# Second attention, first softmax: the best-keys rounds and the low parts of the last two projections' weights moved behind its normalisation on VectorE

## The chip, the cores and the metric

The kernel runs on one core of one Trainium2 chip. The metric is device time in microseconds (us) of the whole launch; the figure for a kernel is the median of several executions. TensorE is called PE (its weight loads PEld), VectorE DVE, ScalarE ACT, GpSimd POOL and SyncE SP.

## The reference, cut to what matters

A block of 256 tokens by 1024 columns passes through a first hybrid layer and then twice (l = 0, 1) through a second layer: attention of two kinds, an output projection with a layer norm, and a routed mixture of 16 experts. The change touches only the attention of the second layer. What it computes, cut down:

```python
proj = h @ w_in                      # split into qa, kva, kr, dq, dk, dv, iq, ik, iw
out_a = mla_group(...)               # 8 heads: softmax(q k^T) v, causal
# dsa_group, 8 heads, per query:
score = sum_heads relu(iq . ik) * iw     # causal
_, sel = lax.top_k(score, 64)            # n_keep = T // 4: the best keys
s = dq . dk[sel] * scale - slopes * dist
out_b = softmax(s) @ dv[sel]
return concatenate([out_a, out_b]) @ w_o
```

## The kernel before, in words

The 256 tokens are two tiles of 128 rows. Every matrix product that must keep float32 accuracy is done in three matmuls, from a high and a low part of each operand: `split` writes the high part on ACT (a rounding copy) and the low part, source minus high, with `lo_of` on DVE or on POOL (line 86 of the profile). The weights' low parts are `hl` tiles in the profile.

In each pass of the second layer, `layer(l)` runs these steps. `proj(0..10)` makes the first eleven column tiles of the input projection, `prep(i)` being the split of tile i's weights. `latent_stats`, `keys`, `values_` and `queries(g)` prepare the four pairs of latent heads. `mla_pair(j)`, j = 0..3, is scores plus `softmax_heads`, called here the first to the fourth softmax. Then `proj(11)` and `proj(12)` make the last two query tiles `dq` for the sparse heads (weights `wb`), `best_keys` finds the 64 best keys of a query in 8 rounds (a maximum of eight and a match-and-replace for each token tile: lines 936 and 937) and turns them into the mask `selm`, and `dsa_pair(j)`, j = 0..3, is the softmax of the sparse heads, which adds `selm` to the scores on PE. The output projection `wo_mm(k)`, k = 0..7, needs the heads of pair k and the split of `wo`'s rows k. Its four accumulators also take the transposed residual (line 83).

`softmax_heads` sets this chain: DVE takes the row maxima from the score sums in PSUM (L390) and scales them (L394); ACT does the exponentials with their sums (L397); DVE takes the reciprocal (L400) and multiplies the probabilities `P` (L402, one half of 128 columns and one of 256 for each head); PE transposes `P` (L406, six matmuls); ACT and DVE copy the transposes to SBUF (L409, L411); PE multiplies with the values (`sc<-P`); ACT and DVE split the result into `oh` and `ol`.

Each engine runs its instructions in the order of its queue, and waits at the first one that isn't ready. The order of each queue is chosen when the program is built, by a list scheduler that interleaves the steps. `with tc.issue_after(ins)` puts the instructions traced in its block behind `ins` on the engine of `ins`; on the other engines it changes nothing directly. `softmax_heads` returns two such marks: `most`, its last maximum (L390), and `first` (returned as `done`), its last multiplication of `P` (L402), both on DVE. The splits of `wo` already stand behind `first` of the first softmax.

`ring` is a ring of SBUF for weights: the first expert's gate weights (line 733) are loaded into the place of `wb`, so their loads wait until `wb` has been read for the last time. All weight loads are issued by SP, in one queue.

A third copy of the layer in the program runs only when an expert has over 64 tokens; it doesn't run here.

Of the kernel before, what the change touches and what calls it, by code (L numbers as in the profile page):

```python
# [34 lines left out]
def body(tc, a, out, dbg=None, upto=None):  # L35
    nc = tc.nc
    te, ve, se, ge, sy = nc.tensor, nc.vector, nc.scalar, nc.gpsimd, nc.sync
# [50 lines left out]
    def split(raw, shape=(1024,), eng=None, tile_=hl8, scale=1.0):  # L88

        t = tile_("hl", F32R, (128, 2, 1024))  # L90
        n = int(np.prod(shape))
        hi, lo = (t[:, i, 0:n] for i in range(2))
        if len(shape) == 2:
            hi, lo = (v.rearrange("p (a b) -> p a b", b=shape[1]) for v in (hi, lo))
        if raw is not None:
            se.activation(hi, raw, AF.Copy, scale=scale)  # L96
            HI["lo"] = lo_of(lo, raw, hi, eng)
        return hi, lo
# [700 lines left out]
    def layer(l, xT, xh, xl, general=False):  # L799
        ex = Experts(l)  # L800

        def wcol(c, n):
            for g, c0, c1 in (("wa", 0, 672), ("wb", 672, 1184), ("wd", 1184, 1312), ("wi", 1312, 1608)):
                if c < c1:
                    return W[f"{g}{l}"][:, :, c - c0:c - c0 + n]
# [17 lines left out]
        def pieces(ps, eng, sc):  # L823
            hi, lo = split(None, (KD, 128))
            for o, n, c in ps:
                se.activation(hi[:, :, o:o + n], wcol(c, n), AF.Copy, scale=sc)
                lo_of(lo[:, :, o:o + n], wcol(c, n), hi[:, :, o:o + n], eng)
            return hi, lo
# [9 lines left out]
        def prep(i):  # L838
            if i < len(tiles) and i not in WS:
                n, j, ps = tiles[i]  # L840
                eng = ge if l and i < 5 or i == 12 else ve
                b = 2 if i < 2 else 1
                sc = behind[:, b:b + 1] if l and i < 5 and not general else 1.0
                WS[i] = pieces(ps, eng, sc) if ps else split(wcol(C0[n] + 128 * j, 128), (KD, 128), eng, scale=sc)

        def proj(i, ahead=1):
            for q in range(ahead + 1):
                prep(i + q)
            if i not in PS:

                both = (0, 1) if i == 0 else (i,)
                for q in both:
                    PS[q] = A("prj", (128, T))
                for k in range(KD):
                    for q in both:
                        wh, wl = WS[q]
                        PS["last"] = mm3(PS[q], wh[:, k], wl[:, k], xh[:, k], xl[:, k], k == 0, k == KD - 1)
            n, j, _ = tiles[i]
            ps = PS[i]
            if n == "iq":  # L860
                se.activation(iq2[:, j, 0], ps, AF.Copy)
                lo_of(iq2[:, j, 1], ps, iq2[:, j, 0])
            elif n == "ikdk":
                for k2, p in ((ik2, ps[0:64]), (dk2, ps[64:128])):
                    for r in (slice(0, 64), slice(64, 128)):
                        se.activation(k2[r, 0], p, AF.Copy)
                        lo_of(k2[r, 1], p, k2[r, 0])
            elif n == "dq":
                se.activation(dq2[:, j, 0], ps, AF.Copy)
                lo_of(dq2[:, j, 1], ps, dq2[:, j, 0])  # L870
            elif n in dest:
                se.activation(dest[n](j), ps, AF.Copy)
            else:
                o = j + (3 if n == "kva" else 0)
                g = V(f"qn{l}" if n == "qa" else f"kvn{l}", j)
                se.activation(nh[:, o], ps, AF.Copy, scale=g)
                ve.scalar_tensor_tensor(out=nl[:, o], in0=ps, scalar=g, in1=nh[:, o].bitcast(F32), op0=ALU.mult, op1=ALU.subtract)
                se.activation(SQ[:, o], ps, AF.Square)
                if j == 1:
                    ge.tensor_tensor(out=SQ[:, o], in0=SQ[:, o], in1=SQ[:, o - 1], op=ALU.add)  # L880
# [52 lines left out]
        def best_keys():  # L933
            for r in range(8):
                for tt, (c, n) in enumerate(SPAN):
                    ve.max(out=m8[:, tt], in_=score[:, c:c + n])
                    ve.match_replace(out=score[:, c:c + n], in_to_replace=m8[:, tt], in_values=score[:, c:c + n], imm_value=-3e38)
            ve.tensor_scalar(score, score, -2e38, NEG, op0=ALU.is_gt, op1=ALU.mult)
            ve.tensor_tensor(out=selm, in0=score, in1=at.maskb, op=ALU.add)
# [72 lines left out]
        def mla_pair(j, S):  # L1012
            return softmax_heads(S, j, rn[:, 2], rn[:, 3, 0:2], lambda s, i: vm[:, s, (2 * j + i) * 64:(2 * j + i) * 64 + 64],
                                 oh[:, j], ol[:, j])
# [32 lines left out]
        first, most = mla_pair(0, S)  # L1047
# [4 lines left out]
        for j in (2, 3):  # L1052
            mla_pair(j, mla_scores(j))

        with tc.issue_after(most.ins):
            best_keys()
        for i in range(11, 13):
            proj(i)
        if not general:
# [360 lines left out]
    for l in range(2):  # L1420
        layer_loads(l)
        state = layer(l, *state)
        if state is None:
            break
        if dbg is not None and upto == f"xo{l}":
            sy.dma_start(dbg, state[0])
            break
    if dbg is None:

        need = nc.values_load(flag[0:1, 0:1], min_val=0, max_val=T)  # L1430
        with tc.If(need > 64):
            xT_ = act("xTg")
            xh_, xl_ = act("xhg", F32R), act("xlg", F32R)
            sy.dma_start(xT_, keep)
            se.activation(xh_, xT_, AF.Copy)
            lo_of(xl_, xT_, xh_)
            state = (xT_, xh_, xl_)
            for l in range(2):
                layer_loads(l, True)
                state = layer(l, *state, general=True)  # L1440
# [76 lines left out]
```

## Time and profile before

| what | value |
|---|---|
| median of 3 executions | 1060.44 us (1060.15 to 1061.89) |
| profiled execution | 1059.44 us |
| its span on the core | 1057.3 us |
| PE busy | 1019.1 us, 96% of the span |
| DVE busy | 531.4 us, 50% |
| ACT busy | 425.6 us, 40% |
| POOL busy | 76.6 us, 7% |
| mean granted clock of PE | 0.996 of full speed |

The profiled execution has its span and 2.1 us around it. Busy time is a mean over stages: the second layer's attention stands at about 405 to 470 us (l = 0) and 752 to 817 us (l = 1) of the span, each followed by the experts.

### The profile page before, as it was taken

The numbers are of one execution on the slowest core, as the hardware profiler recorded it, in microseconds if no ns is written. First come the engines' busy times: TensorE is split into PE (matmuls) and PEld (weight loads), VectorE is DVE, ScalarE is ACT, GpSimd is POOL, SyncE is SP. The second block draws the span as 40 slices with busy tenths as digits, with TensorE's granted clock in tenths as the row PEclk, the third lists the DMA queues.
The fourth block names the chain that finished last, engine by engine and source line by source line (L and its number), as shares of the span: only waits on it lengthen the run. The fifth ranks groups of instructions, "written<-read, shape, count | busy, mean of one in ns | idle before, by whom it ended". The sixth has DMA issues, their size and how long they took to land.

```text
span 1057.3 us, 16626 instructions
## 1 busy us (share of the span) xinstructions
PE 1019.1 (96%) x6768; PEld 730.1 (69%) x6768; DVE 531.4 (50%) x1010; ACT 425.6 (40%) x781; POOL 76.6 (7%) x80
## 2 busy tenths in 40 slices
PE   9999999999999999999899999999999999999995
PEld 7889999999999998775343434379877534343433
DVE  6775578977776679853110111147985402021104
ACT  5675548655554475542110111156654302011111
POOL 3500021000000010001000000032200200000001
PEclk9999999999999999999999999999999999999998
DMA  9933554765444244897999999985469799999995
GB/s 334 349 144 118 200 187 166 249 205 191 160 143 148 95 160 160 296 345 275 389 391 397 399 400 395 391 293 214 160 250 347 280 380 394 400 400 400 394 390 187
DMA packets 131796, 295.41 MB, mean 279 GB/s; under 512 B 6054, under 2 KB 36976, under 8 KB 125440
## 3 DMA queue, kind: packets, MB, share of 16 engines
q1 hardware_dynamic: 129936, 290.35, 74.9%
q0 software_dynamic: 1472, 3.40, 1.1%
q8 instruction: 55, 0.90, 0.3%
q10 hardware_dynamic: 304, 0.53, 0.1%
q14 instruction: 29, 0.24, 0.1%
HBM read 292.15 MB, written 2.10 MB: 278 GB/s over the span
## 4 chain that ended last, share of the span: by engine, by line
PE 85%; DVE 8%; ACT 4%; DMA 1%; issue 1%; POOL 1%; ACTq 0%; DVEq 0%; POOLq 0%
PE gu L74 21%; PE up L74 12%; PE pd L74 11%; PE fm L74 7%; PE prj L74 6%; PE yT L74 6%; PE tm L74 4%; PE wo L74 3%; PE pg L74 3%; PE sum L74 3%; PE sc L74 2%; DVE hl L86 2%; PE sc L406 1%; DMA wa<-in_w_in_dram 1%; ACT P L397 1%
## 5 line engine op out<-in xcount | busy, mean ns | idle before, releaser
L74 PE MATMUL gu<-e,xg 128*64 128x512 f32 x1024 | 226.9, 595 | 1.3 <-ACT sg L1303 1.3
L74 PEld LDWEIGHTS gu<-e,xg 128*64 128x64 f32 x1024 | 71.1, 137 | 134.7 <-issue 128.2
L74 PE MATMUL up<-h2h,hl 128*128 128x256 f32 x704 | 130.5, 283 | 0.0
L74 PE MATMUL pd<-e,aT 128*64 128x512 f32 (+1 forms) x544 | 115.0, 571 | 2.4 <-ACT aT L1318 2.3
L74 PEld LDWEIGHTS up<-h2h,hl 128*128 128x128 f32 x704 | 111.4, 192 | 0.0
L74 PE MATMUL up<-h2l,hl 128*128 128x256 f32 x352 | 99.7, 283 | 0.1
L74 PEld LDWEIGHTS pd<-e,aT 128*64 128x64 f32 x544 | 38.7, 137 | 71.3 <-issue 59.1
L86 DVE TENSOR_TENSOR y<-pd,y 128x512 fp32r<-128x512 f32 (+1 forms) x34 | 21.8, 657 | 104.3 <-ACT y L1334 104.3
L74 PEld LDWEIGHTS up<-h2l,hl 128*128 128x128 f32 x352 | 67.6, 192 | 0.3 <-DVE h2l L522 0.3
L1309 DVE SCALAR_TENSOR_TENSOR sg<-gu,gcol,sg 128x512 f32<-128x512 f32 x16 | 12.0, 751 | 110.0 <-PE gu L74 110.0
L1234 DVE TENSOR_REDUCE gcol<-pgt 64x1 f32<-64x2 f32 x32 | 5.0, 158 | 123.6 <-PE pgt L74 123.4
L74 PE MATMUL yT<-ac,hl 128*128 128x256 f32 x528 | 67.0, 283 | 0.1
L74 PEld LDWEIGHTS yT<-ac,hl 128*128 128x128 f32 x528 | 64.9, 192 | 0.3 <-ACT ac L642 0.3
L86 DVE TENSOR_TENSOR hl<-up,hl 128x1024 fp32r<-128x1024 f32 x44 | 53.8, 1225 | 19.5 <-ACT hl L96 19.4
L96 ACT ACTIVATE hl<-up 128x1024 fp32r<-128x1024 f32 x44 | 46.1, 1052 | 33.8 <-PE up L74 28.4
L1303 ACT ACTIVATE sg<-gu 128x512 f32<-128x512 f32 x16 | 9.6, 598 | 124.0 <-PE gu L74 124.0
L1334 ACT ACTIVATE y<-pd 128x512 fp32r<-128x512 f32 (+1 forms) x34 | 18.8, 571 | 96.1 <-PE pd L74 82.8
L1318 ACT ACTIVATE aT<-pact 128x512 f32<-128x512 f32 x16 | 9.6, 598 | 110.4 <-PE pact L1316 110.4
L74 PE MATMUL fm<-hh,hl 128*128 128x256 f32 x256 | 49.1, 288 | 0.9 <-ACT vu L323 0.9
L86 DVE TENSOR_TENSOR hl<-in,hl 128x1024 fp32r<-128x1024 f32 x32 | 38.6, 1219 | 11.2 <-ACT hl L96 11.0
L74 PE MATMUL wo<-hl,oh 128*128 128x512 f32 x128 | 43.9, 409 | 0.0
L74 PE MATMUL sum<-y,GT 128*128 128x512 f32 (+1 forms) x136 | 38.8, 404 | 3.0 <-ACT y L1334 1.6
(356 smaller groups left out, 2003.3 us busy)
## 6 DMA issues: line engine op xcount, KB each, us to landing
e<-in_w_up_dram SPq DMA_DIRECT2D x48, 1024.0 KB, 13.0
e<-in_w_down_dram SPq DMA_DIRECT2D x48, 1024.0 KB, 13.5
e<-in_w_gate_dram SPq DMA_DIRECT2D x40, 1024.0 KB, 14.5
e<-in_w_gate_dram SPq DMA_DIRECT2D x48, 512.0 KB, 10.8
up<-in_w_up_dram SPq DMA_DIRECT2D x22, 1024.0 KB, 5.2
e<-in_w_up_dram SPq DMA_DIRECT2D x32, 512.0 KB, 10.8
in<-in_w_in_dram SPq DMA_DIRECT2D x15, 1024.0 KB, 17.4
down<-in_w_down_dram SPq DMA_DIRECT2D x11, 1024.0 KB, 5.0
```

The lines of the kernel that those rows point to most:

```text
L74: return te.matmul(o, lhsT=l, rhs=r, start=start, stop=stop, skip_group_check=True)
L86: return (eng or ve).tensor_tensor(out=dst, in0=src, in1=hi.bitcast(F32), op=ALU.subtract)
L96: se.activation(hi, raw, AF.Copy, scale=scale)
L397: se.activation(P[:, i, c:c + n], S[:, i, c:c + n], AF.Exp, scale=scale if isinstance(scale, float) else scale[:, tt:tt + 1], bias=m[:, 1, ...
L406: te.transpose(S[:, i, 128 * b:128 * b + 128], P[:, i, 128 * b:128 * b + 128], ident)
L1234: ve.tensor_reduce(out=gcol[r, p:p + 1], in_=pt[r, x:x + 17:16], axis=AX.X, op=ALU.add)
L1303: se.activation(sg, psg, AF.Silu)
L1309: ve.scalar_tensor_tensor(out=sg, in0=psu, scalar=gcol[:, p:p + 1], in1=sg, op0=ALU.mult, op1=ALU.mult)
L1318: se.activation(aT, pt, AF.Copy)
L1334: se.activation(h_, ps, AF.Copy)
```

## The change

Three edits, which act in both passes. The low part of the weights of `proj(12)` goes from POOL to DVE. The weights' splits of `proj(11)` and `proj(12)`, which were made wherever the scheduler found room before those projections, have their DVE part behind the last multiplication of the first softmax. And `best_keys` stands behind that multiplication, where it stood behind the last maximum of the same softmax.

```diff
@@ prep
-                eng = ge if l and i < 5 or i == 12 else ve
+                eng = ge if l and i < 5 else ve
@@ after the four mla_pair calls
-        with tc.issue_after(most.ins):
+        with tc.issue_after(first.ins):
+            prep(11)
             best_keys()
+            prep(12)
         for i in range(11, 13):
             proj(i)
```

The scheduler makes new queues from this. The rows below are of the first pass; those of the second read alike.

The first place is DVE's queue at the first softmax, behind the last low part of the queries' weights (`hl<-qu`). `sc` is a score tile, `sm` holds a softmax's maxima and sums, `m` the eight best values of a round, `qx` the rotated queries. Before:

```order
L86 TENSOR_TENSOR hl<-wb_3904,hl 128x1024
L390 TENSOR_REDUCE sm<-sc 128x2 x2
L936 MAX m_3882<-score 128x8
L394 TENSOR_TENSOR sm<-sm,rn 128x4
L936 MAX m_3882<-score 128x8
L937 MATCH_REPLACE score<-m_3882,score 128x128
L937 MATCH_REPLACE score<-m_3882,score 128x256
L936 MAX m_3882<-score 128x8 x2
```

The change:

```order
L390 TENSOR_REDUCE sm<-sc 128x2 x2
L394 TENSOR_TENSOR sm<-sm,rn 128x4
L400 RECIPROCAL sm<-sm 128x4
L402 TENSOR_TENSOR P<-P,sm 128x2x128
L402 TENSOR_TENSOR P<-P,sm 128x2x256
L1001 TENSOR_TENSOR qx<-qp,at 128x512
L86 TENSOR_TENSOR hl<-wb_3904,hl 128x1024
L411 COPY P<-sc 128x384
L390 TENSOR_REDUCE sm<-sc 128x2 x2
L936 MAX m_3882<-score 128x8
```

The low part of `proj(11)`'s weights has moved from ahead of the maxima to behind the multiplication, and between the scaled maxima (L394) and the reciprocal (L400), where three rounds of best keys stood, nothing is left. The eight rounds now run between the second softmax's maxima and the fourth softmax's multiplication, all but the last match-and-replace.

The second place is the fourth softmax. First PE's queue around the transposes of its `P` (L406); `sc<-dk,dq` are the scores of the first sparse pair, `prj` is the last projection. Before:

```order
L74 MATMUL wo_4812<-hl,oh 128x512 x2
L74 MATMUL wo_4812<-hl,ol 128x512
L74 MATMUL wo_4813<-hl,oh 128x512
L74 MATMUL sc<-dk_3918,dq_3917 128x2x128 x6
L74 MATMUL sc<-dk_3918,dq_3917 128x256 x6
L406 MATMUL sc<-ident,P 128x128
L74 LDWEIGHTS SQ
L74 MATMUL sc<-at,SQ 128x384
L74 LDWEIGHTS SQ
L74 MATMUL sc<-at,SQ 128x384
L74 LDWEIGHTS identb
L74 MATMUL sc<-selm,identb 128x384
```

The change:

```order
L74 MATMUL sc<-dk_3918,dq_3917 128x2x128 x6
L74 MATMUL sc<-dk_3918,dq_3917 128x256 x6
L74 LDWEIGHTS SQ
L74 MATMUL sc<-at,SQ 128x384
L74 LDWEIGHTS SQ
L74 MATMUL sc<-at,SQ 128x384
L406 MATMUL sc<-ident,P 128x128 x6
L74 MATMUL prj<-xh_3818,hl 128x256 x2
L74 MATMUL prj<-xl_3819,hl 128x256
L74 MATMUL prj<-xh_3818,hl 128x256 x2
L74 MATMUL sc<-P,SQ 64x128 x6
```

Of the last projection's 24 matmuls 22 have moved from ahead of the fourth transposes to behind them; two, which need the high part alone, are still ahead. Eight of the sixteen residual transposes and two matmuls of the output projection have moved behind them too, and the two matmuls `sc<-at,SQ` of the sparse scores have come ahead. And DVE's queue from the fourth softmax's multiplication, in the change:

```order
L402 TENSOR_TENSOR P<-P,sm 128x2x128
L402 TENSOR_TENSOR P<-P,sm 128x2x256
L937 MATCH_REPLACE score<-m_3882,score 128x256
L86 TENSOR_TENSOR hl<-wb_3904,hl 128x1024
L411 COPY P<-sc 128x384
L938 TENSOR_SCALAR score<-score 128x384
L86 TENSOR_TENSOR dq_3917<-prj,dq_3917 128x256
L939 TENSOR_TENSOR selm<-score,at 128x384
L86 TENSOR_TENSOR hl<-wo_3906,hl 128x1024
```

The low part of `proj(12)`'s weights (`hl<-wb`), which POOL made at the time of the first softmax, and the mask `selm` now stand behind the fourth multiplication; before, `selm` stood ahead of it, and so did three low parts of `wo`, which are all behind it now.

The third place is SP's queue, where the first expert loads stand:

```order
+L744 DMA e_4788<-in_w_up_dram 128x4x512
+L744 DMA e_4790<-in_w_up_dram 128x4x512
 L733 DMA e_4780<-in_w_gate_dram 128x2x512
 L733 DMA e_4782<-in_w_gate_dram 128x2x512
 L733 DMA e_4784<-in_w_gate_dram 128x2x512
 L733 DMA e_4786<-in_w_gate_dram 128x2x512
-L744 DMA e_4788<-in_w_up_dram 128x4x512
-L744 DMA e_4790<-in_w_up_dram 128x4x512
```

The four gate loads of half a megabyte, which take the place of `wb`, now stand behind two loads of up weights, and wait for the low part that is made behind the fourth softmax.

## Rows read from the trace of the kernel before

**Rows 1.** The page: the span, and each engine's busy us, share and instructions.

```profile
span 1057.3 us, 16626 instructions
...
PE 1019.1 (96%) x6768; PEld 730.1 (69%) x6768; DVE 531.4 (50%) x1010; ACT 425.6 (40%) x781; POOL 76.6 (7%) x80
```

**Rows 2.** PE's waits in 400:470, then in 745:830: total us, times, longest.

```profile
PE sc L406 <- DVE P L402: 3.2, 4, 2.2
...
PE sc L406 <- DVE P L402: 2.1, 4, 1.1
```

**Rows 3.** PE's timeline, first pass: start us, us, instruction [idle before <-releaser].

```profile
406.47 0.39 PE L74 MATMUL sc<-at,identb 128*128 128x128 bf16 x4
...
411.20 1.48 PE L74 MATMUL sc<-kx,qx 128*128 128x128 f32 x8
414.86 0.30 PE L406 MATMUL sc<-ident,P 128*128 128x128 f32 x1 [2.19 <-DVE P L402]
...
419.20 0.40 PE L74 MATMUL prj<-xh,hl 128*128 128x256 f32 x2
419.44 0.28 PE L74 MATMUL prj<-xl,hl 128*128 128x256 f32 x1
...
431.79 1.31 PE L83 MATMUL wo<-ident,xT 128*128 128x128 f32 x10
432.86 0.71 PE L74 MATMUL wo<-hl,oh 128*128 128x512 f32 x2
...
435.19 0.30 PE L406 MATMUL sc<-ident,P 128*128 128x128 f32 x1 [0.25 <-DVE P L402]
```

**Rows 4.** DVE's timeline, first pass.

```profile
405.79 3.41 DVE L86 TENSOR_TENSOR hl<-wb,hl 128x1024 fp32r<-128x1024 f32 x1
409.12 1.01 DVE L390 TENSOR_REDUCE sm<-sc 128x2 f32<-128x256 f32 x2
...
430.84 0.55 DVE L939 TENSOR_TENSOR selm<-score,at 128x384 bf16<-128x384 f32 x1
431.30 0.75 DVE L86 TENSOR_TENSOR dq<-prj,dq 128x256 fp32r<-128x256 f32 x2
...
433.52 1.20 DVE L86 TENSOR_TENSOR hl<-wo,hl 128x1024 fp32r<-128x1024 f32 x1
434.63 1.02 DVE L402 TENSOR_TENSOR P<-P,sm 128x256 f32<-128x256 f32 x2
435.57 1.22 DVE L86 TENSOR_TENSOR hl<-wo,hl 128x1024 fp32r<-128x1024 f32 x1
```

**Rows 5.** POOL's timeline, the low part of the last projection's weights in each pass.

```profile
405.74 2.37 POOL L86 TENSOR_TENSOR hl<-wb,hl 128x1024 fp32r<-128x1024 f32 x1 [10.93 <-ACT hl L96]
...
753.45 3.46 POOL L86 TENSOR_TENSOR hl<-wb,hl 128x1024 fp32r<-128x1024 f32 x1 [10.65 <-issue]
```

**Rows 6.** DVE's timeline, second pass, at the first softmax.

```profile
755.70 1.22 DVE L394 TENSOR_TENSOR sm<-sm,rn 128x4 f32<-128x4 f32 x1
```

**Rows 7.** Windows: length, busy us by engine, clock, DMA share, GB/s.

```profile
410.00:420.00 10.00, 7.81 (x69) 7.07 (x68) 9.82 (x41) 8.08 (x22) 0.00 (x0) 1.00 0.60 213
...
430.00:440.00 10.00, 9.75 (x81) 7.69 (x80) 9.65 (x19) 5.21 (x15) 0.00 (x0) 1.00 1.02 384
...
480.00:490.00 10.00, 8.71 (x63) 5.80 (x61) 5.27 (x23) 1.13 (x2) 0.00 (x0) 1.00 0.49 156
```

**Rows 8.** ACT's timeline, first pass, at the first softmax's exponentials.

```profile
407.93 0.69 ACT L988 ACTIVATE SQ<-vps,rn 128x512 f32<-128x512 f32 x1 [2.26 <-PE vps L74]
410.43 0.46 ACT L397 ACTIVATE P<-sc,sm,rn 128x128 f32<-128x128 f32 x1 [1.81 <-DVE sm L394]
...
412.88 0.21 ACT L397 ACTIVATION_READ_ACCUMULATOR P<-sc,sm,rn 128x1 f32 x1
```

**Rows 9.** SP's timeline, first pass: the first expert loads.

```profile
409.26 1.90 SPq L733 DMA_DIRECT2D e<-in_w_gate_dram  x4
427.59 3.64 SPq L744 DMA_DIRECT2D e<-in_w_up_dram  x4
```

## The prediction, made before the change was run

> **What bounds the kernel now.** The page comes first: PE is busy for 1019.1 of a span of 1057.3 us [rows 1], so the kernel is as long as PE's work and PE's waits together, and a change to other engines counts only through the waits. The second view is the list of PE's waits over the second layer's attention. In each pass PE waits for one thing alone, the multiplication of `P` on DVE that the transposes need: 3.2 us in four waits in the first pass, 2.1 us in the second [rows 2]. That is all that this change can win, 5.3 us or 0.5%; what it can lose has no such end. Third, the timelines. The largest wait, 2.19 us, is at the first softmax, and another of 0.25 us at the fourth [rows 3]; so 3.2 - 2.19 - 0.25, about 0.7 us, belongs to the sparse pairs. Last, the windows: from 410 to 440 us DVE is busy for 9.7 to 9.8 us of every 10 shown, and PE for nearly as much except at that one wait [rows 7]. Two engines are full here, and the reader should keep both queues in sight.
>
> **Why PE waits at the first softmax.** DVE is late there. It makes the low part of `proj(11)`'s weights just ahead of the maxima, and that instruction takes 3.41 us, where an equal one later takes 1.1 to 1.2 [rows 4]. POOL makes the low part for `proj(12)` at the same moment, 405.74 to 408.11 [rows 5]. In the second pass POOL runs from 753.45 to 756.91, and a DVE instruction on four columns inside that time takes 1.22 us [rows 6]. So POOL's instruction costs DVE some 2.2 us in the first pass and about 1.1 in the second, which is also the difference between the two passes' waits.
>
> **What the change removes.** POOL's instruction is gone, and the low part of 1.1 us no longer stands ahead of the first maxima. These can then start when PE has the scores, at 406.47 + 0.39 = 406.9 [rows 3], instead of 409.12 [rows 4]: 2.2 us earlier. ACT's first exponential still stands behind a copy that begins at 407.93 and takes 0.69 [rows 8], so it starts at 408.6. The four exponentials, with a second such copy among them as before, took from 410.43 to 412.88 + 0.21 = 413.09, 2.66 us [rows 8]; now they end at about 411.3. The first `P` reaches PE at about 412 instead of 414.86, when PE has just come to it, so nearly all of the 2.19 us goes, and of the second pass's wait all but some 0.3.
>
> **What it adds to DVE.** Between the scaled maxima (407.9) and the end of the exponentials (411.3) DVE has nothing to do: three rounds of best keys stood there, and now nothing does. That is 3.4 us of an engine that is full until 440, and the work comes back later. What follows is the fourth multiplication, the last that PE needs before the sparse pairs. Before, DVE worked without a pause from the first maxima at 409.12 to the fourth multiplication at 434.63: 25.5 us [rows 4]. In the new queue this stretch has lost three low parts of `wo` (1.11 each, from 433.52 to 434.63: 3.3), the pass that writes `selm` (430.84 to 431.30: 0.46), two low parts of `dq` (0.7), and the pass before `selm` with the last match-and-replace; these two I estimate at 0.6, since each covers no more columns than the `selm` pass. It has gained one low part of `wb`, 1.1. So 25.5 - 3.3 - 0.5 - 0.7 - 0.6 + 1.1 = 21.5 us of work. The fourth multiplication starts at 406.9 + 21.5 + 3.4 = 431.8, and PE can use it 0.56 us later, as before (434.63 to 435.19) [rows 3, 4]: 432.4.
>
> **What PE has to do until then.** It is earlier than before by 2.8 us at this point, but PE has less to fill the time with. From 411.20 to the wait's start at 434.94 PE did 23.74 - 2.19 = 21.55 us of work [rows 3]. Of this the new queue has moved behind the fourth transposes 22 matmuls of the last projection (0.12 each, from 419.20 to 419.44 for two: 2.6) and 8 residual transposes (0.107 each, ten from 431.79 to 432.86: 0.9) [rows 3]; two matmuls of the output projection and two of the sparse scores change sides and are taken to cancel. That leaves 18.05 us, and PE is through at 429.25. Whatever small waits it meets on the way, it stands at the fourth transposes until 432.4: 3.1 us idle in all.
>
> **The second new wait.** The last projection needs the low part of its weights, which comes behind the fourth multiplication: both halves of `P` take 0.94 (434.63 to 435.57), the last match-and-replace about 0.4 (estimated as above), the low part 1.1 [rows 4]. It is ready at 431.8 + 2.45 = 434.3. PE's six transposes end at about 433.3, held by the second half of `P`; it waits 1.0. Behind the waiting projection in PE's queue stand the values of the fourth softmax, the mask matmuls and all the rest.
>
> **Sum.** New waits 3.1 + 1.0, plus the sparse pairs' 0.7, which I leave as it was: 4.8 us a pass. Against 3.2 in the first pass that is +1.6, against 2.1 in the second +2.7: +4.3 us. The profiled execution has 1057.3 us of span and 2.1 around it, 1059.4; it would become 1063.7. It lies 1.0 below the median of 1060.44, so the median becomes 1064.7, 0.4% more. The hand-offs that the sum leaves out, a wait from one round's result to the next instruction, are between 0 and 1.0 us a pass (DVE showed none before, and dependent pieces now stand closer); I take 0. The sparse pairs' waits lie between 0 and 1.5. The likeliest case's own range is 1061.5 to 1067.5.
>
> A rule of the Trainium skill (Perfetto Trace Analysis, section "Optimizing Scalar/DVE Operations") speaks against this edit by its first half: where DVE is saturated, some of its work may be better on ScalarE or even GpSimd; its second half says that moving work between GpSimd and DVE might not help, as they share a read port. The trace has both sides: DVE full, and a part on POOL that cost DVE 2.2 and 1.1 us where doing it costs 1.1 [rows 4 to 6]. By the first half alone, with the low part on POOL at a harmless time, the second new wait would go and the sum be 1.0 us less a pass, +2.3; by the rows as they stand, the edit to POOL's part is worth 0 to +1.1 us of DVE's time a pass, and the loss comes from the order.
>
> **Loads.** The first gate loads, issued at 409.26 before, now wait for the low part at 434.3, behind two up loads that go at about 427.6 [rows 9]. Two megabytes, 5.5 us at 384 GB/s, move from an idle stretch into a full one (DMA share 1.02 from 430). From 480 to 490 the DMA engines were busy for 0.49 of the time [rows 7], about 5 us free, so the rest of the loads come in time; I price this at 0.
>
> **Rivals.** *Faster*: DVE delivers the fourth `P` before PE needs it, and only the gain at the first softmax is left: about -1.9 in the first pass and -0.8 in the second, 1057.7. It decides from a fourth multiplication at 428.7, 3.1 us earlier than in my sum. For it: every multiplication is earlier than before. Against it: PE arrives earlier still, for the 3.5 us of moved matmuls. *No change*: the delay is taken up behind the attention, since the experts' loads run without pause after 490 and could set the stage's end alone; 1060.4. Against it: those loads wait around 480 to 490 for places that the end of the attention frees, so a late attention makes them late too. It also covers a fourth multiplication half-way between. *Slower still*: the two megabytes can't use that gap, since the loads that stood there come late as well; up to 5.5 us more a pass, 1075.7.
>
> **Chances.** Mine 0.62 (0.55 of it slower by over 0.2%, about 2.1 us, which is what a measurement of this kernel can tell from no change; 0.07 within); faster 0.17 (0.02 of it within); no change 0.15; slower still 0.06. Slower 0.61, within 0.24, faster 0.15. The range goes from 1057.5, which takes in half of the faster case, to 1068.5.
>
> **What would show it.** Right: the first wait of 2.19 gone to under 0.5, DVE idle for some 3 us ahead of the first reciprocal, PE waits of 2 to 3.5 us in front of the third and fourth softmaxes' transposes together and of about 1 us at `prj` for DVE's low part, and 4 to 6 us of PE waits in each pass. Wrong: a fourth multiplication before 429 (then DVE was not the limit), no wait at `prj`, or PE waiting for loads in the experts, which would say that the loads' new place matters.

## The result, and the profile after

| | before | after |
|---|---|---|
| median | 1060.61 us of 6 executions (1059.53 to 1061.89) | 1069.49 us of 6 (1066.76 to 1070.53) |
| profiled execution, its span | 1059.44, 1057.3 us | 1069.24, 1067.4 us |
| mean granted clock of PE | 0.996 | 0.990 |
| the attention, first and second pass | 71.68 and 70.58 us | 76.12 and 76.39 us |

The change costs 8.9 us: the ratio of after to before is 1.0081, 95% interval 1.0069 to 1.0092. The prediction was 1064.7 us in a range of 1057.5 to 1068.5: the direction was right, the size was not. Here "the attention" is the time from the first transposes of `prk` to the first transposes of `z` behind the layer norm, for after 476.20 - 400.08 and 827.89 - 751.50. It has grown by 4.44 and 5.81 us, 10.25 together, where the spans of the two profiled executions differ by 10.1: all of the loss is there. The rest of the span is 0.15 us shorter, which says little, since it is 915.0 us in one execution of the kernel before and 916.7 in another that is shown below; the medians, 8.9 apart, agree with the 10.25 to within that. A ratio here and below is worked out from the executions themselves and is not the quotient of the two medians (1.0084 here).

```profile
400.08 0.38 PE L960 MATMUL prk<-ident,rn 128*128 128x128 f32 x2
...
476.20 1.03 PE L772 MATMUL pt<-ident,z 128*128 128x128 f32 x8
...
751.50 0.38 PE L960 MATMUL prk<-ident,rn 128*128 128x128 f32 x2
...
827.89 0.82 PE L772 MATMUL pt<-ident,z 128*128 128x128 f32 x6
```

The page of after, its rows of PE: the same number of instructions, but 1026.7 us of busy time instead of 1019.1 [rows 1]. PE didn't only wait longer, it worked longer, and the clock's row shows two dips that the page of before hasn't got.

```profile
span 1067.4 us, 16620 instructions
...
PE 1026.7 (96%) x6768; PEld 735.2 (69%) x6768; DVE 530.2 (50%) x1012; ACT 425.3 (40%) x781; POOL 70.7 (7%) x78
...
PEclk9999999999999999899999999999989999999998
```

PE's waits of after from 400 to 470 us (us in total, times, longest), which answer to [rows 2]:

```profile
PE sc L406 <- DVE P L402: 2.2, 4, 1.4
PE sc L74 <- DVE ol L86: 0.9, 1, 0.9
PE prj L74 <- DVE hl L86: 0.8, 1, 0.8
PE sc L74 <- DVE P L411: 0.6, 1, 0.6
```

Four kinds of wait where there was one, 4.5 us where there were 3.2; the second pass has the same four, 4.5 where there were 2.1. DVE's timeline of after shows why; it answers to [rows 4]:

```profile
407.09 1.02 DVE L390 TENSOR_REDUCE sm<-sc 128x2 f32<-128x256 f32 x2 [1.03 <-PE sc L74]
...
411.39 0.18 DVE L400 RECIPROCAL sm<-sm 128x4 f32<-128x4 f32 x1 [3.08 <-ACT P L397]
...
432.13 1.02 DVE L402 TENSOR_TENSOR P<-P,sm 128x256 f32<-128x256 f32 x2
...
433.46 1.22 DVE L86 TENSOR_TENSOR hl<-wb,hl 128x1024 fp32r<-128x1024 f32 x1
```

The maxima start 2 us earlier, DVE stands idle for 3.08 us where the rounds had been, the fourth softmax's multiplication comes at 432.13, and behind it the low part of the last projection's weights. PE's timeline of after, which answers to [rows 3]:

```profile
412.17 0.30 PE L406 MATMUL sc<-ident,P 128*128 128x128 f32 x1 [0.17 <-DVE P L402]
...
428.04 0.88 PE L74 MATMUL sc<-P,SQ 128*64 128x128 f32 x12 [0.64 <-DVE P L411]
429.86 0.98 PE L74 MATMUL sc<-dk,dq 64*128 64x256 f32 x12 [0.94 <-DVE ol L86]
...
432.69 0.30 PE L406 MATMUL sc<-ident,P 128*128 128x128 f32 x1 [1.43 <-DVE P L402]
433.20 0.77 PE L406 MATMUL sc<-ident,P 128*128 128x128 f32 x5 [0.21 <-DVE P L402]
434.73 0.80 PE L74 MATMUL prj<-xh,hl 128*128 128x256 f32 x2 [0.76 <-DVE hl L86]
...
436.09 1.55 PE L74 MATMUL sc<-P,SQ 128*64 128x128 f32 x12
```

The first wait of 2.19 is down to 0.17. From 427.4 on PE waits five times within 7.3 us. Then look at the durations: the twelve matmuls `sc<-P,SQ` take 0.88 us at 428.04 and 1.55 at 436.09. The windows of one us show the reason (after the two bounds: width, PE busy, PEld, DVE, ACT, POOL, granted clock, DMA share, GB/s):

```profile
431.00:432.00 1.00, 0.27 (x2) 0.00 (x0) 1.00 (x6) 0.42 (x2) 0.00 (x0) 1.00 0.89 313
...
433.00:434.00 1.00, 0.77 (x5) 0.53 (x5) 1.00 (x4) 0.00 (x0) 0.00 (x0) 1.00 1.05 410
434.00:435.00 1.00, 0.27 (x1) 0.27 (x2) 1.00 (x2) 0.49 (x1) 0.00 (x0) 0.56 0.54 207
435.00:436.00 1.00, 1.00 (x5) 0.87 (x5) 1.00 (x4) 0.00 (x0) 0.00 (x0) 0.50 0.33 33
...
439.00:440.00 1.00, 1.00 (x7) 1.00 (x6) 0.66 (x1) 0.00 (x0) 0.00 (x0) 0.50 0.97 358
440.00:441.00 1.00, 1.00 (x7) 1.00 (x6) 0.00 (x0) 0.00 (x0) 0.00 (x0) 0.53 0.96 356
441.00:442.00 1.00, 1.00 (x11) 0.64 (x12) 0.20 (x1) 0.62 (x2) 0.00 (x0) 1.00 0.80 299
```

From 434.1 to 440.9 the granted clock is 0.50, 1.2 instead of 2.4 GHz, and PE, busy all the time from 435, gets through seven matmuls in each of the last two us, and through eleven in the first us after the clock is back. In the second pass's windows the same stands from 785.7 to 792.5. Before, the clock was 1.00 here [rows 7]. These windows are of one execution, but the fall is not that execution's alone: the mean granted clock of the whole span is 0.988 to 0.992 in all six executions of after, and 0.992 to 0.996 in the executions of the kernel before that were run beside the kernels below.

### The profile page after: what moved, and what is told of

Its sections match the earlier page's. It is cut to its first block, busy times and chain, and to the rows that moved or that the text cites. A ratio compares the mean times of both kernels' runs of the same rounds, so it can differ in the third digit from the quotient of the medians.

```text
span 1067.4 us, 16620 instructions
## 1 busy us (share of the span) xinstructions
PE 1026.7 (96%) x6768; PEld 735.2 (69%) x6768; DVE 530.2 (50%) x1012; ACT 425.3 (40%) x781; POOL 70.7 (7%) x78
## 4 chain that ended last, share of the span: by engine, by line
PE 78%; DMA 9%; DVE 7%; ACT 3%; issue 1%; POOL 1%; SPq 0%; ACTq 0%; DVEq 0%; POOLq 0%
PE gu L74 16%; PE up L74 12%; PE pd L74 8%; PE fm L74 7%; PE prj L74 6%; PE yT L74 6%; PE tm L74 4%; PE wo L74 4%; DMA e<-in_w_up_dram 3%; PE sc L74 3%; PE pg L74 3%; DMA e<-in_w_gate_dram 2%; DMA e<-in_w_down_dram 2%; PE sum L74 2%; PE qp L74 1%; PE sc L406 1%
## 5 line engine op out<-in xcount | busy, mean ns | idle before, releaser
L74 PE MATMUL prj<-xhn,hl 128*128 128x256 f32 x208 | 41.4, 296 | 2.2 <-POOL hl L86 1.0
```

The lines of the kernel that those rows point to most:

```text
L74: return te.matmul(o, lhsT=l, rhs=r, start=start, stop=stop, skip_group_check=True)
```

## The experiments

Theory A: the change costs some 2 us a pass in waits, as predicted, and nearly 3 more by the clock that falls behind them. Rival B: the new place of the gate loads, or the attention's new order itself, costs the time. Question C: what does each part of the change do alone? Lengths of the attention are taken as above from each kernel's profiled execution, of which there is one for each kernel; a median stands beside its ratio to the kernel before, run on the same chip (before's median lay between 1060.52 and 1060.86 us).

| kernel | attention, us | median, us | ratio (95%) |
|---|---|---|---|
| before | 71.68, 70.58 | 1060.6 | |
| after | 76.12, 76.39 | 1069.49 | 1.0081 (1.0069 to 1.0092) |
| after, all waits filled, transposes | 73.43, 73.63 | 1065.34 | 1.0037 (1.0026 to 1.0047) |
| after, all waits filled, matmuls | 73.42, 73.59 | 1066.50 | 1.0049 (1.0032 to 1.0066) |
| after, the fourth softmax's wait filled | 73.43, 73.61 | 1065.54 | 1.0039 (1.0026 to 1.0053) |
| after, the other waits filled | 74.61, 74.86 | 1065.74 | 1.0050 (1.0036 to 1.0063) |
| before, gate loads late | 71.64, 70.57 | 1063.19 | 1.0021 (1.0010 to 1.0032) |
| engine's part alone | 69.53, 69.55 | 1057.11 | 0.9960 (0.9946 to 0.9973) |
| order's part alone | 71.75, 71.73 | 1062.70 | 1.0013 (1.0003 to 1.0023) |
| both low parts behind the first softmax, rounds not | 70.78, 70.78 | 1060.47 | 0.9994 (0.9984 to 1.0003) |
| low parts first, then the rounds | 71.46, 71.47 | 1061.52 | 1.0004 (0.9993 to 1.0016) |

**All waits filled.** The fillers are put into PE's finished queue, ahead of the instructions at which it waits, so that no other instruction changes its place (`u`: ahead of the third softmax's products with the values; `v`: behind them; `t`: ahead of the fourth softmax's transposes; `p`: ahead of the last projection's third matmul; `warm` is the instruction that is copied, here a transpose of the identity).

```diff
+            FILLS.append((MARK["p"], (u, 5, 0), (v, 8, 1), (t, 12, 0), (MARK["p"], 6, 0)))
...
+            for _ in range(count):
+                f = copy.replace(warm, name=nc.get_next_instruction_name(), outs=[copy.replace(o, offset=o.offset + 256, ap=warm.outs[0].ap)])
+                code.insert(at, f)
```

> The changed kernel with 31 transposes of the identity a pass put into PE's own waits (5, 8, 12 and 6 of them, into a free half of the last projection's bank): they compute nothing that is used, every other instruction keeps its place. Theory A (the waits cost 3.9 us and the fall of the granted clock to 0.50 behind them about 6): PE has no cluster of waits left, the granted clock stays at 1.00 from 430 to 445, the projection's matmuls go at 0.12 us again instead of 0.21, and the time is 1063 to 1064.5, 3 to 4 above the kernel before. Rival B (the loads' new place, or the attention's new order itself, costs the 9 us and the clock only marks where PE waits): 1069 to 1070, as the change. If the clock stays up and the time is still 1069, A falls.

Measured: 1065.34 us, 0.8 above the expected range, and the attention is 2.69 and 2.76 us shorter than after's, with the clock at 1.00 in it. The waits are no shorter, they are only full: the fourth softmax's multiplication starts 32.07 us behind the first transposes of `prk`, in after 32.05. (This kernel's sums are not those of after: its fillers probably spoil the first two products of the last projection, which no run tested by itself.) So I repeated it with other fillers, copies of the last projection's second matmul, `q`:

```diff
+            FILLS.append((MARK["q"], (u, 5, 0), (v, 7, 1), (t, 11, 0), (MARK["p"], 6, 0)))
```

> The changed kernel again with fillers in PE's waits, here 29 extra matmuls a pass (5, 7, 11 and 6, each a copy of the last projection's second matmul at 0.12 us) into the unused half of that projection's bank; nothing that is used changes, and every other instruction keeps its place. Theory A, with the size that the first filled kernel gave (waits +1.7 and +3.1 over the attention's two passes, the clock 2.7 us a pass): clock 1.00 from 430 to 445, attention 63.7 and 63.9 us long instead of 66.4 and 66.7, 1064 to 1066. If the first filled kernel gained because its transposes spoiled part of the projection, this one is back at 1069.

(The expectation counts the attention from a later mark; its 66.4 and 63.7 us stand for 76.1 and 73.4 here.) Measured: 73.42 and 73.59 us, the same within 0.04. The median is 0.5 above the expectation. More work on PE makes the changed kernel faster by 0.3 to 0.4%: that shows the clock's share, 2.7 to 2.8 us a pass, and it refutes B's second half: the order is that of after, and the time is not.

**One place filled, and its complement.** The two edits are against the kernel with all waits filled with matmuls.

```diff
-            FILLS.append((MARK["q"], (u, 5, 0), (v, 7, 1), (t, 11, 0), (MARK["p"], 6, 0)))
+            FILLS.append((MARK["q"], (u, 0, 0), (v, 0, 1), (t, 11, 0), (MARK["p"], 0, 0)))
```

> The same fillers in one place only: 11 matmuls ahead of the fourth softmax's transposes, where the longest wait (1.43 us) is; the waits of 0.64, 0.94 and 0.76 us stay open. Theory A1 (any long wait of the cluster lowers the clock): it stays at 1.00 once the longest is filled, 1064 to 1066. Theory A2 (the waits count together, however they are divided): 2.5 us of waits within 7 us are still left, the clock falls for part of the time or not at all, between 1065 and 1069. Rival B: 1069.

Measured: 73.43 and 73.61. Its windows, and below them its waits from 400 to 470 us, show a PE that still stands idle for 3 us, at full clock throughout:

```profile
433.00:434.00 1.00, 0.79 (x6) 0.53 (x5) 1.00 (x4) 0.00 (x0) 0.00 (x0) 1.00 1.01 393
434.00:435.00 1.00, 0.24 (x2) 0.18 (x2) 1.00 (x2) 0.49 (x1) 0.00 (x0) 1.00 0.61 234
435.00:436.00 1.00, 1.00 (x13) 0.87 (x15) 1.00 (x4) 0.00 (x0) 0.00 (x0) 1.00 0.28 31
```

```profile
PE sc L93 <- DVE ol L105: 0.9, 1, 0.9
PE sc L425 <- DVE P L421: 0.8, 3, 0.4
PE prj L93 <- DVE hl L105: 0.8, 1, 0.8
PE sc L93 <- DVE P L431: 0.6, 1, 0.6
```

This is the cleanest measure of the terms. It leaves 3 us of true waits open, the attention is 1.75 and 3.03 us longer than before, and after is 2.69 and 2.78 us longer still (the clock's price). The 1.75 and 3.03 are not all waits. The windows of the whole attention, first pass, of before, of after and of this kernel:

```profile
399.89:471.57 71.68, 68.43 (x504) 55.80 (x503) 57.85 (x144) 36.77 (x100) 2.37 (x1) 1.00 0.73 269
400.08:476.20 76.12, 71.54 (x504) 58.51 (x503) 56.78 (x145) 36.80 (x100) 0.00 (x0) 0.96 0.63 233
400.17:473.60 73.43, 70.15 (x515) 57.46 (x514) 56.72 (x145) 36.84 (x100) 0.00 (x0) 1.00 0.66 241
```

PE idles for 71.68 - 68.43 = 3.25 us before and for 76.12 - 71.54 = 4.58 in after, so the waits cost 1.3 us (2.4 in the second pass). Here it idles for 3.28, as the fillers work in the other 1.3; without them 68.85 us of work are left, 0.4 more than before at the same clock (0.55 in the second pass). That is PE's own work in its new order, and what makes it longer isn't settled. So the first pass's 4.44 us are 1.33 of waits, 0.40 of the order and 2.71 of the clock, and the second's 5.81 are 2.44, 0.55 and 2.82. The medians of after and of this kernel differ by 4.0 us, where the attentions differ by 5.5; that, too, is within what the rest of the span varies by.

```diff
+            FILLS.append((MARK["q"], (u, 5, 0), (v, 7, 1), (t, 0, 0), (MARK["p"], 6, 0)))
```

> The complement of the kernel with one filled place: fillers in the three shorter waits (5, 7 and 6 matmuls into 0.64, 0.94 and 0.76 us), none ahead of the fourth softmax's transposes, where 1.43 and 0.21 us stay open. Theory A1 (the long wait alone lowers the clock): it falls as in the change, attention 4.4 and 5.8 us longer than before, 1069. Theory A2 (only the waits together do it, as the kernel before, with one wait of 2.19 us, shows no fall): clock at 1.00, attention 1.7 and 3.0 us longer, 1064 to 1066.

Measured: neither. The attention is 2.93 and 4.28 us longer than before, and the clock falls for half as long, from 432.2 to 435.6:

```profile
431.00:432.00 1.00, 0.27 (x1) 0.14 (x1) 1.00 (x4) 0.00 (x0) 0.00 (x0) 1.00 0.87 322
432.00:433.00 1.00, 0.79 (x5) 0.76 (x5) 1.00 (x4) 0.00 (x0) 0.00 (x0) 0.59 1.05 410
433.00:434.00 1.00, 1.00 (x6) 1.00 (x5) 0.71 (x1) 0.40 (x1) 0.00 (x0) 0.50 0.53 205
434.00:435.00 1.00, 1.00 (x6) 1.00 (x6) 0.87 (x3) 0.10 (x1) 0.00 (x0) 0.50 0.12 27
435.00:436.00 1.00, 1.00 (x9) 0.86 (x9) 1.00 (x3) 0.00 (x0) 0.00 (x0) 0.70 0.92 276
```

In these profiled executions the wait of 1.42 us alone brings a short fall, all waits together a long one, the short ones alone none. But before has a wait of 2.19 us in this stage and no fall. So neither the longest wait nor their sum decides by itself; what does stays open. The median, from five executions, is no higher than that of the filled kernels; here only the profile tells them apart, and whether every execution has the short fall isn't shown: the mean granted clock of the span is 0.993 to 0.995 in the five, and 0.993 to 0.996 in those with the fourth softmax's wait filled.

**The loads' place, by itself.** In the kernel before, the first gate load of each pass waits for a later value of DVE's semaphore.

```diff
+        load = next(i for i in code if type(i).__name__ == "InstDMACopy" and str(i.outs[0].memref).startswith(tile_name))
+        code[code.index(load)] = copy.replace(load, sync_info=copy.replace(load.sync_info, on_wait=[
+            copy.replace(w, wait_value=count) if w.ant_name.startswith("DVE") else w for w in load.sync_info.on_wait]))
```

> The kernel before with one wait made longer: the first of the four gate loads of each pass waits on DVE for the fourth softmax's multiplication (434.6 instead of 409.3 us), so the four loads, and the up loads queued behind them, are issued where the change issues the gate loads or later. Nothing else moves. Theory A: within 1 us of 1060.6, since the stretch from 480 to 490 us has 5 us of idle DMA time. Rival B (the loads' place costs): 2.5 to 5.5 us a pass, 1066 to 1071.

Measured: 1063.19 us, more than A allows and less than B asks for. SP's timeline of this kernel shows that the loads are as late as meant, the up loads far later than in the change:

```profile
436.71 1.90 SPq L754 DMA_DIRECT2D e<-in_w_gate_dram  x4
438.72 6.19 SPq L765 DMA_DIRECT2D e<-in_w_up_dram  x4
```

The attention has its old length, and between 470 and 760 us PE's list of waits is that of before, with no load in it. From the first transposes of `z` to the second pass's transposes of `prk` it takes 749.43 - 472.54 = 276.89 us instead of 275.96, and behind the second pass's first transposes of `z` 1.5 us more; in both stretches the clock falls to 0.50, from 506.9 to 510.3 and from 855.1 to 858.5 us, where the profiled execution of before has 1.00.

> The kernel before once more, for the spread between executions of one program. The kernel with the late loads lost 0.9 and 1.5 us outside the attention, where its clock fell to 0.50 at 506 and near 850 us behind waits that the kernel before has too. If that belongs to executions and not to the loads, this execution may show such a fall as well, with a time of up to 1063; if it shows none, the cause stays open.

Measured: 1061.54 us, ratio 1.0007 (0.9996 to 1.0017), and this execution does show the fall at 506. First its windows of two us, then those of the kernel before:

```profile
504.00:506.00 2.00, 0.74 (x4) 0.56 (x4) 1.04 (x2) 0.29 (x1) 0.00 (x0) 1.00 1.02 378
506.00:508.00 2.00, 1.64 (x4) 0.49 (x6) 0.47 (x2) 0.31 (x1) 0.00 (x0) 0.61 1.02 377
508.00:510.00 2.00, 2.00 (x8) 0.68 (x6) 0.00 (x0) 0.00 (x0) 0.00 (x0) 0.53 1.04 400
510.00:512.00 2.00, 2.00 (x12) 0.60 (x10) 0.00 (x0) 0.00 (x0) 0.00 (x0) 1.00 1.05 379
```

```profile
502.00:504.00 2.00, 1.30 (x8) 0.14 (x2) 0.56 (x1) 0.00 (x0) 0.00 (x0) 1.00 1.02 325
504.00:506.00 2.00, 1.07 (x6) 0.76 (x8) 0.95 (x3) 0.60 (x1) 0.00 (x0) 1.00 0.96 322
506.00:508.00 2.00, 2.00 (x12) 0.70 (x10) 0.00 (x0) 0.00 (x0) 0.00 (x0) 1.00 1.01 367
```

PE is busy for 10.37 of the 12 us from 500 in both; in one execution the clock falls behind the gap, in the other not. So such a fall needs no late loads. That they make it more frequent (2.2 us on average, by the ratio) was not excluded. For the change itself B's first half is out as the price of the attention: the filled kernels have the late gate loads (434.83 us with the fourth wait filled, 434.74 in after), and their attention's loss is that of the waits and of PE's order. Behind the attention a cost of up to about 2 us is not excluded.

**The parts alone.**

```diff
-                eng = ge if l and i < 5 or i == 12 else ve
+                eng = ge if l and i < 5 else ve
```

> One part of the change alone: the low part of the last projection on DVE instead of GpSimd; the best keys' rounds stay behind the first maxima. Theory A: the low part of projection 11 takes 1.1 us instead of 3.4, the maxima start 2.2 us earlier, the first wait of 2.19 (1.09) us nearly goes, DVE stays full, no cluster of waits, granted clock 1.00: 1056 to 1058.5. Rival C (DVE is full, so another 1.1 us on it comes back as a wait at the fourth softmax or at the projection): 1059.5 to 1061.5.

Measured: 1057.11 us, faster than before by 0.40%. DVE's timeline, and then PE's only wait of the first pass:

```profile
406.35 1.22 DVE L86 TENSOR_TENSOR hl<-wb,hl 128x1024 fp32r<-128x1024 f32 x1
407.48 1.01 DVE L390 TENSOR_REDUCE sm<-sc 128x2 f32<-128x256 f32 x2
...
424.65 1.20 DVE L86 TENSOR_TENSOR hl<-wb,hl 128x1024 fp32r<-128x1024 f32 x1
```

```profile
PE sc L406 <- DVE P L402: 0.4, 1, 0.4
```

The low part of projection 11 takes 1.22 instead of 3.41 us [rows 4], the maxima follow at once, and the rounds fill the time in which ACT does the exponentials. The other low part, 1.2 us at 424.65, delays nobody. The attention is 2.15 and 1.03 us shorter; the waits were 3.2 and 2.1 [rows 2] and are 0.4 and 0.4. The gate loads are issued at 426.35 us here, 17 later than before, and the kernel is faster all the same.

The order's part alone is the change with the condition `or i == 12` put back:

> The other part alone: rounds and the low part of projection 11 behind the first normalisation, the low part of projection 12 left on GpSimd at its old time. The wait at the projection for DVE goes, and its 24 matmuls can stand ahead of the fourth transposes again; DVE still idles for some 3 us. Theory A: waits of 2 to 4 us a pass in all, fewer of them close together, so the clock stays at 1.00 or falls for less time: 1059 to 1064. If the waits are as after and the clock falls as after, 1067 to 1069. Rival B (loads): the gate loads go at 409 again, so the time is that of before, 1060, whatever the waits do.

Measured: 1062.70 us, attention +0.07 and +1.15, the clock at 1.00 in it. PE's waits are 1.8 us a pass, none over 0.8. The last projection's weights are ready early here, and its matmuls stand ahead of the fourth transposes, in the place of the largest wait. So the waits are shorter than before's 3.2 and 2.1, and yet nothing is won: by the windows of the attention PE is busy for 69.86 and 69.84 us with the same matmuls, where it was for 68.43 in each pass. The loss of this kernel is PE's own work in another order, 1.4 us a pass.

Two other orders, with both low parts on DVE:

```diff
         with tc.issue_after(first.ins):
             prep(11)
-            best_keys()
             prep(12)
+        with tc.issue_after(most.ins):
+            best_keys()
```

> Both low parts of the last projections behind the first normalisation on DVE, as in the change, but the best keys' rounds back behind the first maxima, so that they fill DVE's idle 3.2 us. Theory A: DVE is full, no cluster of waits, the clock at 1.00: 1055.5 to 1058.5, as the kernel with the engine's part alone (1057.1). Rival: the low parts come late for PE, which reaches the projections by 415 us, and PE waits there for 1 to 2 us a pass: 1059 to 1061.

Measured: 1060.47 us, a miss: no change. The rival's time came, but not its waits. Only 0.35 us of waits a pass are left, yet the attention gains 0.90 us in the first pass and loses 0.20 in the second. With no more wait than the kernel with the engine's part alone it takes 1.2 us longer a pass. The windows of the attention, first pass, here and with the engine's part alone, say where:

```profile
401.66:472.44 70.78, 70.27 (x504) 55.96 (x502) 56.29 (x145) 36.66 (x100) 0.00 (x0) 1.00 0.68 249
400.45:469.98 69.53, 69.09 (x504) 56.02 (x503) 56.62 (x145) 36.52 (x100) 0.00 (x0) 1.00 0.67 247
```

The same matmuls at the same clock keep PE busy for 1.2 us longer. Its queue is interleaved in another way, with the last softmax's values at 466.7 us instead of 461.1; why that costs PE time wasn't settled.

```diff
             prep(11)
-            best_keys()
             prep(12)
+            best_keys()
```

> The change with the second low part ahead of the rounds instead of behind them. DVE still idles for 3.2 us, but the last projection's matmuls can stand ahead of the fourth transposes and fill PE's time. Theory A: the wait at the projection goes, the fourth multiplication stays late by about 1 us, 1.5 to 3 us of waits a pass, not close together, clock at 1.00: 1060 to 1063.5. If the clock falls all the same: 1064 to 1067. Rival B (the gate loads, which go some 15 us earlier here, were the cost): 1060 or less even if the waits are as in the change.

Measured: 1061.52 us, no change. Attention -0.22 and +0.89, 2.5 us of waits a pass in four places, clock at 1.00. The gate loads go early here and nothing is won by it beyond the waits, which speaks against B once more.

## Why the prediction was wrong

**Right: what the change does to DVE and to the waits.** The maxima start when PE has the scores (predicted 406.9, came 407.09). The first wait goes from 2.19 to 0.17 us. DVE idles for 3.08 us ahead of the reciprocal (predicted 3.4). The fourth multiplication, worked out by adding and taking away DVE's instructions, was put at 431.8 and came at 432.13, of which 0.2 is there from the span's start. The waits of 3.1 us ahead of the fourth transposes came as 0.64 + 0.94 + 1.43 + 0.21 = 3.22, in four places: some of PE's earlier instructions hang on DVE too, for which the prediction had left room. By its own sign, 2 to 3.5 us in front of the transposes themselves, it is a miss, since 1.64 stand there. The wait at the projection was predicted at 1.0 and took 0.76, the sparse pairs' waits 0.7 and took 0.41. Sum: 4.8 us a pass predicted, 4.6 measured. (One reading is a little off: DVE wasn't quite without a pause from 409.12 to 434.63 before; it waited 0.21 us for ACT ahead of 430.36.)

**Right: that the new waits add up to about +4.3 us.** They cost 1.33 + 2.44 = 3.8 us. With the clock held at 1.00 by one filled place the attention is 1.75 + 3.03 = 4.78 us longer than before, and the median 1065.54 us; 1064.7 was predicted. That this comes so near owes something to luck: 0.95 of the 4.78 are PE's own work in its new order, which the sum doesn't have.

**Wrong: the sum took PE's work as unchanged.** The step that failed is "PE has less to fill the time with" and the sum behind it: it priced the idle time and let the matmuls behind it keep their durations of before, 0.12 us each. After five waits in 7.3 us they ran at half the clock for 6.8 us in each pass. The missing term is 2.69 + 2.78 = 5.5 us, more than the +4.3 that was predicted for the waits; the new order's 0.40 and 0.55 us of PE's work, at full clock, are missing beside it. The windows of before that stand beside the prediction have a granted clock of 1.00 [rows 7], and it never asks whether the clock would stay there. The Trainium skill (TensorE: Matmul & The Clock Gate, section "A second HAM failure mode: psum-queue depth-cycling") tells of another kernel whose PE idles briefly between groups of matmuls, there by its cycling through the banks of PSUM, often enough that its clock goes back and forth between its two levels, and throughput suffers. The trace agrees in kind, with 0.50 from 434.1 to 440.9 us behind five short waits, once in each pass. It should have been a rival with a chance of its own.

**Right: the loads at nothing, for the change.** No PE wait for a load appeared behind the attention, and the delay came through one to one, within the 1.7 us by which the rest of the span differs between two executions of before. Of the rivals, faster and no change are refuted. The slower rival, with up to 1075.7 us, takes in the measured time, but by a mechanism that did not act.

**The engine's edit was undervalued.** The prediction gave it 0 to 1.1 us of DVE's time a pass. Alone it is worth 2.15 and 1.03 us on PE's path, since the low part that DVE takes over falls where nobody waits for it. By the first half of the rule weighed there the prediction put the change without the engine's edit at +2.3 us instead of +4.3. The order's part alone came to 1.0013, +1.4 us, for another reason than the one worked out: the projection's matmuls moved into the wait, the waits fell to 1.8 us a pass, and PE's own work grew by 1.4. With the engine's part alone 3.41 us become 1.22 once POOL is quiet, and the kernel is 0.40% faster. The Trainium skill (Perfetto Trace Analysis, section "Optimizing Scalar/DVE Operations") says that moving work between GpSimd and DVE might not help, since they share a read port. The trace agrees that the two get in each other's way, though no row shows a port; here the move to DVE did help. That the loss isn't the engine's edit was right; that it comes from the order holds only with that edit beside it, since the order alone costs 1.4 us of the 8.9.

## What to carry to other kernels

On an engine whose clock can fall behind its waits, a new wait has two prices: the idle time, and the slower work behind it. When a change leaves several waits within a few us of dense matmuls, ask whether PE has other work that is ready to stand there; here eleven extra matmuls a pass in the longest wait took 5.5 us off the two attentions. A new order can also change the time that PE needs for the same matmuls: at full clock it went from 68.4 to 70.3 us a pass among these kernels, so compare PE's busy time as well as its waits. And test the parts of a change apart: the engine's edit alone wins 0.4%, where both together lose 0.8%.

## What the hardware showed unexpectedly

The granted clock fell behind waits that one execution of a program had with the fall and another without it: 10.37 us busy of 12 from 500 us in both, and a fall to 0.50 from 506.4 to 509.9 us in one alone. A wait of 2.19 us brought no fall in the attention of before; in the profiled executions one of 1.42 us brought 3.4 us of it in the changed kernel, and with the shorter waits around it 6.8 us.

While POOL writes its low part, DVE's maxima, which read PSUM, keep their duration: 1.02 us at 408.15 in the kernel with the order's part alone, beside POOL's instruction from 407.00 to 409.38, and 1.02 in after without it. The low part that took 3.41 us beside POOL [rows 4, 5] reads and writes SBUF. There POOL's instruction began first, at 405.74, and took 2.37 us; in the second pass of before DVE's began first, at 753.43, 0.02 us ahead, and it was POOL's that took longer: 1.22 us on DVE, 3.46 on POOL [rows 5].
